# Turning the normalised residual: scaled rows and transposes in place of diagonal float32 matmuls

## The chip, the cores and the metric

The kernel runs on one core of a Trainium2 chip. The metric is the device time of one execution in microseconds (us); the time before is the median of three executions. A profile of one further execution gives the trace that the rows below come from. The engines are called PE (TensorE), DVE (VectorE), ACT (ScalarE), POOL (GpSimd) and SP (SyncE), as in the profile.

## The reference

One decoder layer over 2048 tokens of width 1024, all in float32. Two attention groups run side by side (stick-breaking attention with 8 heads, gated linear attention with 4), their outputs go through an output projection and are added to the residual, and a feed-forward part with a short convolution follows:

```
x = x + concat([o_sb, o_gla], axis=-1) @ w_out       # output projection, residual
h = rms_norm(x, ffn_norm_g)                          # x * rsqrt(mean(x*x) + 1e-6) * g
u = causal_depthwise_conv(h @ w_ffn_up, conv_w, conv_b)   # 1024 -> 5632, width 3
a, val = split(u, 2, axis=-1)
x = x + (silu(a) * val) @ w_ffn_down                 # 2816 -> 1024
return rms_norm(x, final_norm_g)
```

The change lies in how `h` is made from `x` and handed to the up-projection.

## The kernel before

**Precision.** Large products are computed with each float32 operand split into a high and a low part of type float32r (`split_psum` L92, `split_w` L101): ACT writes the high part out of PSUM (L94, or L97 with a scale per partition), and DVE writes the difference as the low part (L95, L98). A product is then three matmuls (high x high, high x low, low x high), as in the up-projection at L881 to L883, called ups here.

**Stages.** A first stage projects the input and stores queries, keys and values in DRAM. After it, `ffn(b, ...)` (L812) runs once for each of four blocks b of 512 tokens. For a block it runs the output projection (`accumulate`, L728), the norm and the turn to feature-major form (L839 to L854, the place of the change), the up-projection with convolution, and the down-projection (again `accumulate`).

**What runs between.** `ffn` is a generator. Each `yield` hands out an amount of the program's own clock, and a loop at the end of the kernel issues attention work for later blocks as that clock advances: one step of `attention_steps` (L506) whenever `done < clock / SPAN * total`, with SPAN = 1030 and total = 296. A step is, on PE, two matmuls that add to the attention output (acc, L581 and L582), four transposes of weights (tp, L566) and two matmuls for scores (z, L533); on ACT two sigmoids (into mt and wt) and the high part of the transposed weights (ws); on DVE a scan (L549), a product (L555) and the low part of ws (L95). Steps are used up before block 3's place of the change, so none stands there.

**Order.** PE's instructions stand in the order in which the program writes them (`manual_schedule` for PE). The order on DVE, ACT, POOL and SP is found by a scheduler from the dependencies. Engines wait for each other by semaphores. A tile that takes a named buffer (a `slot`, or one of the four PSUM banks of pool `pc` with tag "c") waits until the readers of the buffer's last tile are done.

**The place itself.** The last three rows of the output projection are staggered by token tile (128 tokens each): for t = 0 to 3, PE does the nine matmuls of tile t, DVE adds the residual into x1 (L786), ACT squares and sums the row (L789), DVE adds the two half sums (L795) and POOL raises the result to -0.5 (L799), which gives the scale r1 of tile t. After `yield FILL` (4.0), DVE multiplies the 128x128 identity by r1 for each t (dg, L846). Then, for each of the eight feature tiles k, PE multiplies the four x1 pieces (128 tokens x 128 features) with the four diagonal matrices (L851, plain float32), which scales and transposes them into one PSUM bank (tpu), and ACT and DVE write h2h and h2l from it, scaled by the feature gain g (L97, L98). h2h and h2l are two buffers each, of four feature tiles: slots 10 and 11, and 14 and 15. They are allocated once, in block 0. Each k ends with `yield 0.9`.

Of the kernel before, what the change touches and what calls it, by code (L numbers as in the profile page):

```python
# [8 lines left out]
F32 = mybir.dt.float32  # L9
F32R = mybir.dt.float32r  # L10
AF = mybir.ActivationFunctionType
ALU = mybir.AluOpType
# [4 lines left out]
P = 128  # L17
D = 1024
KT = D // P
S = 2048  # L20
TB = 512
# [29 lines left out]
def hybrid_block_kernel(ctx, tc, x, attn_norm_g, w_in, w_gate_up, b_gate_up, sb_out_g,  # L51
                        gla_out_g, w_out, ffn_norm_g, w_ffn_up, conv_w, conv_b,
                        w_ffn_down, final_norm_g, out):
    nc = tc.nc
# [4 lines left out]
    out = out[0]  # L59
# [4 lines left out]
    ident = const.tile([P, P], F32, name="ident")  # L64
# [27 lines left out]
    def split_psum(hi, lo, ps, scale=None):  # L92
        if scale is None:
            nc.scalar.activation(hi, ps, AF.Copy)  # L94
            nc.vector.tensor_tensor(out=lo, in0=ps, in1=hi.bitcast(F32), op=ALU.subtract)  # L95
        else:
            nc.scalar.activation(hi, ps, AF.Identity, scale=scale)  # L97
            nc.vector.scalar_tensor_tensor(out=lo, in0=ps, scalar=scale, in1=hi.bitcast(F32),  # L98
                                           op0=ALU.mult, op1=ALU.subtract)
# [10 lines left out]
    pc = ctx.enter_context(tc.tile_pool(name="pc", bufs=4, space=PSUM))  # L110

    def slot(n, shape, dtype, name):
        return big.tile(shape, dtype, tag=f"slot{n}", name=name)
# [4 lines left out]
    if True:  # L118
        c1.enter_context(tc.tile_pool(name="rpad", bufs=1, side="right")).tile([P, 24], F32, name="rpad")

        def w_tile(shape, dtype, name):
            return low.tile(shape, dtype, tag="w", name=name, bufs=4)
# [17 lines left out]
        for n in (6, 7, 8, 9, 10, 11, 14, 15, 0, 1, 2, 3, 4, 5, 12, 13):  # L140
            b, u = n // 4, n % 2
# [84 lines left out]
        with tc.tile_pool(name="lr", bufs=2, side="right") as lp, tc.tile_pool(name="lc", bufs=1, side="right") as lc:  # L226
# [16 lines left out]
            for b in range(NB):  # L243
# [11 lines left out]
                for j in range(NPAIR):  # L255
# [12 lines left out]
                                                 op0=ALU.mult, op1=ALU.add)  # L268
# [4 lines left out]
                                            in0=bcn[:, :, P - 1:P].to_broadcast([P, 4, P]), in1=bcn,  # L273
# [15 lines left out]
                                                   op0=ALU.mult, op1=ALU.mult)  # L289
# [127 lines left out]
        n = 0  # L417
# [270 lines left out]
    cc = ctx.enter_context(tc.tile_pool(name="cc", bufs=1))  # L688
# [13 lines left out]
    halo = [cc.tile([P, 2 * NCH, 2], F32, name=f"halo{i}") for i in range(2)]  # L702
    hadd = cc.tile([P, 2 * NCH, 2], F32, name="hadd")
    x1 = [slot(12 + u, [P, 2, D], F32, f"x1_{u}") for u in range(2)]
    h2h, h2l = [], []
    ur = Ring([w_tile([P, 2, KT, P], F32R, f"u{n}") for n in range(3)])
    d01 = w_tile([P, 2, 2, 512], F32R, "d01")
    dr = Ring([d01[:, 0], d01[:, 1], m1_tile([P, 2, 512], F32R, "d2")])
# [5 lines left out]
    def x1t(t):  # L714
        return x1[t // 2][:, t % 2, :]
# [96 lines left out]
    def ffn(b, oT, rows, nextT):  # L812
# [15 lines left out]
        if b == 0:  # L828
# [5 lines left out]
        rs1, rs2 = ([r[:, t:t + 1] for t in range(4)] for r in (r1, r2))  # L834
        last = b + 1 == NB
        yield from accumulate(oT, w_out, wou, b, squares=sq1, stagger=True, rstds=[r1], rows=rows,
                              extra=previous if b > 0 else remaining, first=None if b > 0 else ahead)
        if b == 0:
            h2h.extend(slot(10 + u, [P, 4, TB], F32R, f"h2h{u}") for u in range(2))  # L839
            h2l.extend(slot(14 + u, [P, 4, TB], F32R, f"h2l{u}") for u in range(2))  # L840
        yield FILL

        dgs = []
        for t in range(4):
            dg = cc.tile([P, P], F32, tag=f"dg{t}", name="dg")
            nc.vector.tensor_scalar(out=dg, in0=ident, scalar1=rs1[t], scalar2=None, op0=ALU.mult)  # L846
            dgs.append(dg)
        for k in range(KT):
            tp = pc.tile([P, 4, P], F32, tag="c", name="tpu")
            for t in range(4):  # L850
                nc.tensor.matmul(tp[:, t, :], x1t(t)[:, k * P:(k + 1) * P], dgs[t], start=True, stop=True)  # L851
            split_psum(h2h[k // 4][:, k % 4, :], h2l[k // 4][:, k % 4, :], tp.rearrange("p t q -> p (t q)"),
                       scale=g_f[:, k:k + 1])
            yield 0.9  # L854
        hcur, hprev = halo[b % 2], halo[(b + 1) % 2]
        if b > 0:
            nc.vector.tensor_tensor(out=hadd[:, :, 0], in0=hprev[:, :, 0], in1=cw[:, 0, :], op=ALU.mult)
# [6 lines left out]
        for gi, G in enumerate(GROUPS):  # L864
            gts = []
            for c in range(ch0, ch0 + G):
                cs = []
                for s in range(2):
# [17 lines left out]
                    n = s * NCH + c  # L886
# [73 lines left out]
    for b in range(NB):  # L960
        nextT = []
        for dt in ffn(b, oT, order if b == 0 else None, nextT):
            clock += dt
            while done < total and done < clock / SPAN * total:
                next(later, None)
                done += 1
        assert b + 1 == NB or done >= need[b + 1]
        oT = nextT
# [27 lines left out]
```

## Time and profile before

| | |
|---|---|
| median of three executions | 2766.29 us (2762.18 to 2768.05) |
| the profiled execution | 2762.93 us |
| its span in the trace | 2761.2 us |
| PE busy | 2696.3 us, 98% |
| DVE busy | 1686.7 us, 61% |
| ACT busy | 1146.3 us, 42% |
| POOL busy | 610.7 us, 22% |
| mean granted clock of PE | 0.996 |

The profiled execution is 1.7 us longer than its span; those lie around the instructions. The granted clock is a share of PE's full speed: 1.00 is the higher of its two levels (2.4 GHz), 0.50 the lower (1.2 GHz). The matmuls of PE overlap, and the duration given for one matmul is a latency; the distance between the starts of two neighbours says more.

### The profile page before, as it was taken

How to read it: one execution, taken by the hardware profiler on the slowest of the kernel's cores; microseconds unless marked ns; L12 is line 12 of the kernel's file. 1: busy time of each engine (PE TensorE's matmuls, PEld its weight loads, DVE VectorE, ACT ScalarE, POOL GpSimd, SP SyncE). 2: the span in 40 equal slices, each digit the busy share in tenths (PEclk: the TensorE clock that was granted, in tenths of full speed). 3: DMA queues.
4: the chain of work that ended last, by engine and by line, in shares of the span. 5: the costliest groups of instructions: out<-in, count | busy, mean ns of one | idle time of the engine just before them, and what ended most of it. 6: DMA issues, size and time to landing. Idle time of an engine off the chain costs nothing.

```text
span 2761.2 us, 36066 instructions
## 1 busy us (share of the span) xinstructions
PE 2696.3 (98%) x13000; PEld 2235.0 (81%) x13000; DVE 1686.7 (61%) x2777; ACT 1146.3 (42%) x2371; POOL 610.7 (22%) x937
## 2 busy tenths in 40 slices
PE   8999999999899899999999999999999999999998
PEld 7878888878688778887888888888888888888887
DVE  5246755457677687777776877777867334242333
ACT  5455533335465455554543444445434222220112
POOL 2001212214555555543111111111110000000000
PEclk9999999999999999999999999999999999999999
DMA  6215644477667677768455555574554656555552
GB/s 193 91 62 175 231 143 150 126 180 238 237 226 256 223 240 258 241 232 279 156 185 183 177 172 176 185 253 151 179 176 151 232 191 218 206 197 191 198 190 84
DMA packets 254563, 526.92 MB, mean 191 GB/s; under 512 B 54864, under 2 KB 143024, under 8 KB 231856
## 3 DMA queue, kind: packets, MB, share of 16 engines
q1 hardware_dynamic: 223136, 387.76, 42.8%
q0 software_dynamic: 31104, 136.33, 13.7%
q8 instruction: 102, 1.67, 0.2%
q14 instruction: 77, 0.63, 0.1%
q10 hardware_dynamic: 144, 0.52, 0.1%
HBM read 382.99 MB, written 141.56 MB: 190 GB/s over the span
## 4 chain that ended last, share of the span: by engine, by line
PE 85%; DVE 5%; DMA 4%; POOL 2%; ACT 2%; issue 2%; SPq 1%; ACTq 0%; POOLq 0%; DVEq 0%
PE ups L881 11%; PE ups L882 11%; PE ups L883 11%; PE d L760 6%; PE d L759 6%; PE d L761 6%; PE z L533 4%; PE tp L566 4%; PE mm L170 2%; PE mm L169 2%; PE mm L168 2%; PE acc L582 2%; PE mm L179 2%; PE mm L180 2%; PE mm L178 2%; PE acc L581 2%
## 5 line engine op out<-in xcount | busy, mean ns | idle before, releaser
L881 PE MATMUL ups<-h2h,u 128*128 128x512 f32 x1408 | 552.2, 392 | 3.9 <-DVE x L786 3.9
L882 PE MATMUL ups<-h2l,u 128*128 128x512 f32 x1408 | 551.0, 391 | 0.0
L883 PE MATMUL ups<-h2h,u 128*128 128x512 f32 x1408 | 550.3, 391 | 0.0
L881 PEld LDWEIGHTS ups<-h2h,u 128*128 128x128 f32 x1408 | 265.1, 188 | 60.5 <-DVE x L786 4.4
L883 PEld LDWEIGHTS ups<-h2h,u 128*128 128x128 f32 x1408 | 264.9, 188 | 57.2
L95 DVE TENSOR_TENSOR ws<-tp,ws 128x512 fp32r<-128x512 f32 (+1 forms) x320 | 193.8, 606 | 191.9 <-ACT ws L94 191.0
L882 PEld LDWEIGHTS ups<-h2l,u 128*128 128x128 f32 x1408 | 265.0, 188 | 55.5
L759 PE MATMUL d<-d,g 128*128 128x512 f32 x736 | 290.9, 395 | 4.2 <-DVE x L786 1.8
L94 ACT ACTIVATE ws<-tp 128x512 fp32r<-128x512 f32 (+1 forms) x320 | 170.2, 532 | 299.9 <-PE tp L566 295.5
L760 PE MATMUL d<-d,g 128*128 128x512 f32 x736 | 289.3, 393 | 1.5 <-POOL d L103 1.5
L761 PE MATMUL d<-d,g 128*128 128x512 f32 x736 | 288.7, 392 | 0.0
L893 DVE SCALAR_TENSOR_TENSOR ct<-ups,cwb,ct 128x511 f32<-128x511 f32 x176 | 131.7, 748 | 249.2 <-POOL ct L892 196.2
L888 ACT ACTIVATE ct<-ups,cwb 128x512 f32<-128x512 f32 x176 | 136.3, 775 | 340.3 <-PE ups L883 340.1
L549 DVE TENSOR_TENSOR_SCAN wtB<-mt,cy 128x512 f32<-128x512 f32 x192 | 248.4, 1294 | 3.1 <-ACT mt L538 3.0
L786 DVE TENSOR_TENSOR x<-d,x 128x512 f32<-128x512 f32 x128 | 85.8, 683 | 166.1 <-PE d L761 166.0
L892 POOL TENSOR_TENSOR ct<-ct,hadd 128x2 f32<-128x2 f32 x132 | 26.4, 200 | 688.7 <-ACT halo L890 324.5
L538 ACT ACTIVATE mt<-z 128x512 f32<-128x512 f32 (+2 forms) x320 | 170.5, 533 | 9.4 <-DVE cy L553 5.1
L759 PEld LDWEIGHTS d<-d,g 128*128 128x128 f32 x736 | 138.7, 189 | 36.0 <-DVE x L786 3.4
L760 PEld LDWEIGHTS d<-d,g 128*128 128x128 f32 x736 | 138.6, 188 | 31.8 <-POOL d L103 2.5
L761 PEld LDWEIGHTS d<-d,g 128*128 128x128 f32 x736 | 138.5, 188 | 30.9
L168 PE MATMUL mm<-hh,w 128*128 128x512 f32 x384 | 151.2, 394 | 0.0
L170 PE MATMUL mm<-hh,w 128*128 128x512 f32 x384 | 149.4, 392 | 0.8 <-POOL w L103 0.8
(262 smaller groups left out, 5375.4 us busy)
## 6 DMA issues: line engine op xcount, KB each, us to landing
u<-wup SPq DMA_DIRECT2D x132, 1024.0 KB, 4.7
d<-wdn SPq DMA_DIRECT2D x94, 512.0 KB, 3.4
wup<-u POOLq DMA_DIRECT2D x44, 1024.0 KB, 6.6
kvA<-kvs POOLq DMA_DIRECT2D x52, 512.0 KB, 4.8
uraw<-in_w_ffn_up_dram SPq DMA_DIRECT2D x44, 512.0 KB, 4.6
wdn<-d POOLq DMA_DIRECT2D x44, 512.0 KB, 5.2
d<-wou SPq DMA_DIRECT2D x38, 512.0 KB, 4.3
dw<-wdn SPq DMA_DIRECT2D x38, 512.0 KB, 4.2
```

What stands on the lines that cost most here:

```text
L94: nc.scalar.activation(hi, ps, AF.Copy)
L95: nc.vector.tensor_tensor(out=lo, in0=ps, in1=hi.bitcast(F32), op=ALU.subtract)
L168: nc.tensor.matmul(ps, whi[k][:, fs], hh[b][k // 4][:, k % 4, :], start=(k == 0), stop=False)
L170: nc.tensor.matmul(ps, wlo[k][:, fs], hh[b][k // 4][:, k % 4, :], start=False, stop=(k == KT - 1))
L538: nc.scalar.activation(m[:, lo:TB], z[:, :width], AF.Sigmoid, scale=-0.125)
L549: nc.vector.tensor_tensor_scan(out=pp[:, ::-1], data0=mr, data1=mr, initial=1.0 if prev is None else prev, op0=ALU.mult, op1=ALU.bypass)
L759: nc.tensor.matmul(accs[t], gh[:, ts], whi, start=(ci == 0), stop=False)
L760: nc.tensor.matmul(accs[t], gh[:, ts], wlo, start=False, stop=False)
L761: nc.tensor.matmul(accs[t], gw[:, ts], whi, start=False, stop=(ci == G - 1))
L881: nc.tensor.matmul(ps, whi[:, k, :], hk, start=(k == 0), stop=False)
L882: nc.tensor.matmul(ps, whi[:, k, :], lk, start=False, stop=False)
L883: nc.tensor.matmul(ps, wlo[:, k, :], hk, start=False, stop=(k == KT - 1))
```

## The change

The identity is no longer scaled. DVE instead scales the residual rows themselves: for each token tile t and each half u of the 1024 features, x1 is multiplied by r1 of the tile into a new tile xn[u] (128x512 float32, eight instructions a block). PE then transposes the 128x128 pieces of xn with the identity, and `split_psum` follows as before. Three further things move with it:

- xn[0] and xn[1] take slots 11 and 15, which before held h2h's and h2l's second half. The second half of h2h and h2l is therefore allocated anew in each block, and it waits until the transposes of the xn in its slot have been done.
- For the first four feature tiles, PE does the transposes of token tiles 0 to 2 first, twelve of them into all four banks of `pc`, and those of token tile 3 behind them. `split_psum` of each of the four tiles follows on its last transpose.
- The yields are 4.0, 1.3, 0.5 and four times 0.5, where they were 4.0 and eight times 0.9.

```
-        if b == 0:
-            h2h.extend(slot(10 + u, [P, 4, TB], F32R, f"h2h{u}") for u in range(2))
-            h2l.extend(slot(14 + u, [P, 4, TB], F32R, f"h2l{u}") for u in range(2))
+        h2h = [slot(10, [P, 4, TB], F32R, "h2h0"), None]
+        h2l = [slot(14, [P, 4, TB], F32R, "h2l0"), None]
+
+        xn = [slot(n, [P, 4, D // 2], F32, f"xn{u}") for u, n in enumerate((11, 15))]
+        for t in range(4):
+            for u in range(2):
+                nc.vector.tensor_scalar(out=xn[u][:, t, :], in0=x1t(t)[:, u * 512:(u + 1) * 512], scalar1=rs1[t],
+                                        scalar2=None, op0=ALU.mult)
         yield FILL
 
-        dgs = []
-        for t in range(4):
-            dg = cc.tile([P, P], F32, tag=f"dg{t}", name="dg")
-            nc.vector.tensor_scalar(out=dg, in0=ident, scalar1=rs1[t], scalar2=None, op0=ALU.mult)
-            dgs.append(dg)
-        for k in range(KT):
-            tp = pc.tile([P, 4, P], F32, tag="c", name="tpu")
-            for t in range(4):
-                nc.tensor.matmul(tp[:, t, :], x1t(t)[:, k * P:(k + 1) * P], dgs[t], start=True, stop=True)
+        def turn(tp, k, ts_):
+            for t in ts_:
+                nc.tensor.transpose(tp[:, t, :], xn[k // 4][:, t, (k % 4) * P:(k % 4 + 1) * P], ident)
+
+        def parts(tp, k):
             split_psum(h2h[k // 4][:, k % 4, :], h2l[k // 4][:, k % 4, :], tp.rearrange("p t q -> p (t q)"),
                        scale=g_f[:, k:k + 1])
-            yield 0.9
+
+
+        tps = [pc.tile([P, 4, P], F32, tag="c", name="tpu") for _ in range(KT // 2)]
+        for k, tp in enumerate(tps):
+            turn(tp, k, range(3))
+        yield 1.3
+        for k, tp in enumerate(tps):
+            turn(tp, k, (3,))
+            parts(tp, k)
+        h2h[1] = slot(11, [P, 4, TB], F32R, "h2h1")
+        h2l[1] = slot(15, [P, 4, TB], F32R, "h2l1")
+        yield 0.5
+        for k in range(KT // 2, KT):
+            tp = pc.tile([P, 4, P], F32, tag="c", name="tpu")
+            turn(tp, k, range(4))
+            parts(tp, k)
+            yield 0.5
```

How the instructions stand now is shown for block 2. The number behind a name tells tiles of one name apart. In the program before, PE's order from the last attention step ahead of the turn into the turn is this: the end of a step (its two acc matmuls, four transposes tp, two score matmuls z), then four diagonal matmuls for each feature tile, four tiles in a row (the first two are shown whole here).

```order
L581 MATMUL acc_16466<-ws0_5042,kvA_5057 128x512
L582 MATMUL acc_16466<-ws0_5042,kvA_5057 128x512
L566 MATMUL tp_16846<-ident_60,wtC_5513 128x128 x2
L566 MATMUL tp_16846<-ident_60,wtA_5055 128x128 x2
L533 MATMUL z_16855<-kvA_5057,qA_5058 128x128 x2
L851 MATMUL tpu_16876<-dg_16868,x1_0_6295 128x128
L851 MATMUL tpu_16876<-dg_16870,x1_0_6295 128x128
L851 MATMUL tpu_16876<-dg_16872,x1_1_6296 128x128
L851 MATMUL tpu_16876<-dg_16874,x1_1_6296 128x128
L851 MATMUL tpu_16883<-dg_16868,x1_0_6295 128x128
L851 MATMUL tpu_16883<-dg_16870,x1_0_6295 128x128
```

Behind the fourth tile, before, another whole step stands on PE, and then the other four tiles. Now, behind the step, PE has the twelve and the four transposes of feature tiles 0 to 3, two tiles from xn1, a step, the last two tiles, and the first ups matmul (L897, which was L881):

```order
L849 MATMUL tpu_16850<-ident_60,xn0_16822 128x128 x3
L849 MATMUL tpu_16851<-ident_60,xn0_16822 128x128 x3
L849 MATMUL tpu_16848<-ident_60,xn0_16822 128x128
L849 MATMUL tpu_16849<-ident_60,xn0_16822 128x128
L849 MATMUL tpu_16850<-ident_60,xn0_16822 128x128
L849 MATMUL tpu_16851<-ident_60,xn0_16822 128x128
L849 MATMUL tpu_16878<-ident_60,xn1_16823 128x128 x4
L849 MATMUL tpu_16885<-ident_60,xn1_16823 128x128 x4
L581 MATMUL acc_16526<-ws1_5043,kvA_5057 128x512
L582 MATMUL acc_16526<-ws1_5043,kvA_5057 128x512
```

The step that stood behind the fourth tile stands behind the sixth now, and all sixteen transposes of the first four tiles are in one piece ahead of it. On DVE, before, the stretch from the low part of the transposed weights (ws0) to the first h2l of block 2 reads so (r1 is the sum of squares of the last token tile):

```order
L95 TENSOR_TENSOR ws0_5042<-tp_16830,ws0_5042 128x512
L795 TENSOR_TENSOR r1_16341<-sq1_16340 128x1
L549 SCALAR_TENSOR_TENSOR wtB_5056<-mt1_5035,cy_16691 128x512
L846 TENSOR_SCALAR dg_16874<-ident_60,r1_16341 128x128
L555 TENSOR_TENSOR wtC_5513<-wtC_5513,wtB_5056 128x512
L95 TENSOR_TENSOR ws1_5043<-tp_16846,ws1_5043 128x512
L549 SCALAR_TENSOR_TENSOR wtB_5056<-mt0_5034 128x128
L98 SCALAR_TENSOR_TENSOR h2l0_6810<-tpu_16876,g_f_6285,h2h0_6808 128x512
```

And now, from the residual sum x1_1 of the last token tile's second half to the first h2l (L785 and L794 are the lines that were L786 and L795):

```order
L785 TENSOR_TENSOR x1_1_6296<-d3_16592,x1_1_6296 128x512
L843 TENSOR_SCALAR xn0_16822<-x1_1_6296,r1_16305 128x512
L843 TENSOR_SCALAR xn1_16823<-x1_1_6296,r1_16305 128x512
L555 TENSOR_TENSOR wtA_5055<-wtA_5055,wtB_5056 128x512
L95 TENSOR_TENSOR ws0_5042<-tp_16806,ws0_5042 128x512
L794 TENSOR_TENSOR r1_16305<-sq1_16304 128x1
L549 SCALAR_TENSOR_TENSOR wtB_5056<-mt1_5035,cy_16663 128x512
L843 TENSOR_SCALAR xn0_16822<-x1_1_6296,r1_16305 128x512
L843 TENSOR_SCALAR xn1_16823<-x1_1_6296,r1_16305 128x512
L555 TENSOR_TENSOR wtA_5055<-wtA_5055,wtB_5056 128x512
L95 TENSOR_TENSOR ws1_5043<-tp_16834,ws1_5043 128x512
L549 SCALAR_TENSOR_TENSOR wtB_5056<-mt0_5034,cy_16694 128x512
```

Behind the last of these stand one more product (L555) and the first h2l. The small dg has gone; two scalings of 128x512 stand in its place, two more ahead of ws0, and the scan behind ws1 is a full one of 512 columns, where a scan of 128 stood.

## Rows read from the trace of the kernel before

**Rows 1.** Page, busy time of the engines: busy us (share of span) xinstructions.

```profile
PE 2696.3 (98%) x13000; PEld 2235.0 (81%) x13000; DVE 1686.7 (61%) x2777; ACT 1146.3 (42%) x2371; POOL 610.7 (22%) x937
```

**Rows 2.** Windows (us; busy of PE, PEld, DVE, ACT, POOL; PEclk; DMA; GB/s).

```profile
746.87:764.22 17.35, 13.42 (x98) 11.84 (x97) 17.11 (x25) 12.89 (x25) 10.62 (x12) 1.00 0.50 167
...
1330.67:1344.57 13.90, 12.72 (x97) 11.55 (x96) 12.37 (x25) 10.59 (x21) 5.09 (x9) 1.00 0.42 148
...
1896.24:1909.49 13.25, 12.52 (x98) 11.30 (x96) 12.95 (x24) 10.05 (x21) 2.97 (x7) 1.00 0.61 197
...
2383.38:2392.77 9.39, 7.58 (x65) 7.20 (x64) 5.84 (x10) 5.45 (x9) 1.03 (x2) 1.00 0.45 164
```

**Rows 3.** Lines by form: count | busy us, mean ns | idle us before, releaser.

```profile
L566 PE MATMUL tp<-ident,wtA 128*128 128x128 f32 x520 | 97.6, 273 | 1.6 <-DVE wtA L555 1.6
...
L851 PE MATMUL tpu<-dg,x 128*128 128x128 f32 x256 | 30.9, 276 | 4.3 <-DVE dg L846 4.3
...
L549 DVE TENSOR_TENSOR_SCAN wtB<-mt,cy 128x512 f32<-128x512 f32 x192 | 248.4, 1294 | 3.1 <-ACT mt L538 3.0
...
L95 DVE TENSOR_TENSOR ws<-tp,ws 128x512 fp32r<-128x512 f32 x224 | 153.8, 687 | 169.1 <-ACT ws L94 168.3
...
L555 DVE TENSOR_TENSOR wtA<-wtA,wtB 128x512 f32<-128x512 f32 x107 | 77.8, 727 | 5.1 <-DVE wtB L549 0.9
...
L98 DVE SCALAR_TENSOR_TENSOR h2l<-tpu,g_f,h2h 128x512 fp32r<-128x512 f32 x32 | 23.0, 743 | 2.5 <-ACT h2h L97 1.3
...
L383 DVE TENSOR_SCALAR og<-po,grr 128x128 f32<-128x128 f32 x64 | 19.4, 344 | 12.0 <-POOL grr L89 11.9
...
L264 DVE TENSOR_SCALAR la<-mm,bgate 128x512 f32<-128x512 f32 x8 | 6.0, 746 | 13.6 <-ACT e L260 13.6
```

**Rows 4.** One line's instructions, L846: count, min/median/max ns, first and last start.

```profile
L846 DVE TENSOR_SCALAR dg<-ident,r x16: 256/278/1497, 739.3 to 2385.9; 128x128 f32<-128x128 f32 x16
```

**Rows 5.** Timeline, blocks 1 and 3: start us, us, engine, work [idle before <-releaser].

```profile
1339.15 1.45 ACT L97 ACTIVATE h2h<-tpu,g_f 128x512 fp32r<-128x512 f32 x2
...
2385.93 0.29 DVE L846 TENSOR_SCALAR dg<-ident,r 128x128 f32<-128x128 f32 x1 [0.66 <-POOL r L799]
...
2386.80 0.69 ACT L97 ACTIVATE h2h<-tpu,g_f 128x512 fp32r<-128x512 f32 x1 [1.72 <-PE tpu L851]
```

**Rows 6.** Timeline of block 2, around the diagonal matmuls.

```profile
1898.26 0.68 DVE L95 TENSOR_TENSOR ws<-tp,ws 128x512 fp32r<-128x512 f32 x1
...
1899.00 0.50 PE L582 MATMUL acc<-ws,kvA 128*128 128x512 f32 x1 [0.51 <-DVE ws L95]
...
1902.01 0.73 DVE L98 SCALAR_TENSOR_TENSOR h2l<-tpu,g_f,h2h 128x512 fp32r<-128x512 f32 x1
...
1903.52 0.48 PE L581 MATMUL acc<-ws,kvA 128*128 128x512 f32 x1
...
1904.06 0.38 PE L566 MATMUL tp<-ident,wtA 128*128 128x128 f32 x2
...
1904.74 2.84 PE L851 MATMUL tpu<-dg,x 128*128 128x128 f32 x24
...
1907.19 2.06 DVE L98 SCALAR_TENSOR_TENSOR h2l<-tpu,g_f,h2h 128x512 fp32r<-128x512 f32 x3
```

**Rows 7.** Timeline of block 0, around the last dg.

```profile
753.35 1.50 DVE L846 TENSOR_SCALAR dg<-ident,r 128x128 f32<-128x128 f32 x1
...
753.48 1.27 POOL L103 TENSOR_TENSOR d<-draw,d 128x512 fp32r<-128x512 f32 x1
...
754.90 3.17 PE L851 MATMUL tpu<-dg,x 128*128 128x128 f32 x26 [2.47 <-DVE dg L846]
```

**Rows 8.** Timeline of block 0, an ups matmul behind an idle time of PE.

```profile
947.57 0.50 PE L881 MATMUL ups<-h2h,u 128*128 128x512 f32 x1 [3.94 <-DVE x L786]
```

**Rows 9.** Windows behind two idle times of PE, columns as in rows 2.

```profile
948.00:952.00 4.00, 4.00 (x13) 3.14 (x12) 3.40 (x6) 0.00 (x0) 2.50 (x4) 0.60 0.93 320
...
755.00:759.00 4.00, 4.00 (x34) 3.86 (x35) 3.88 (x6) 2.95 (x5) 0.57 (x1) 1.00 0.96 305
```

More of the change, by code (lines that the diff above doesn't have):

```diff
@@ L704, in hybrid_block_kernel @@
     x1 = [slot(12 + u, [P, 2, D], F32, f"x1_{u}") for u in range(2)]
-    h2h, h2l = [], []
     ur = Ring([w_tile([P, 2, KT, P], F32R, f"u{n}") for n in range(3)])
```

## The prediction

> **What bounds the kernel now.** I read the page first: TensorE (PE) is busy for 98% of the span [rows 1], so in most places a microsecond of PE work taken away is a microsecond won. The change touches one place only, which comes four times, once per block of 512 tokens: the turn of the normalised residual into feature-major operands, between the last output-projection matmul and the first up-projection matmul (ups). So next I cut those four stretches out of the trace [rows 2]. Each label runs from the issue of the first PE instruction behind the last projection matmul to the issue of the first ups matmul. The reader is to see three things there. The stretches last 17.35, 13.90, 13.25 and 9.39 us, 53.9 together. PE idles in them for 3.9, 1.2, 0.7 and 1.8 us (length less busy time). And VectorE (DVE) is busy for 17.11 of 17.35, 12.37 of 13.90 and 12.95 of 13.25 us in the first three: in this place two engines are full, not one. Block 3 has no attention work left to run beside it, and there DVE has 3.5 us of air.
>
> **What is removed: PE time.** The diagonal matmuls are 8 x 4 per block, 128 in the program, but the trace has 256 of them [rows 3]: a float32 matmul runs as two passes. 24 take 2.84 us [rows 6]; the last one's 0.27 us of modelled tail off, that is 2.57/23 = 0.112 us each, so 256 x 0.112 = 28.6 us. A transpose is one instruction: two in 0.38 us [rows 6] is a pitch of 0.38 - 0.27 = 0.11 us (the means of 273 and 276 ns in [rows 3] are latencies and hide this). 128 x 0.11 = 14.1 us. So PE loses 14.5 us of work, 3.6 per block. If nothing came back, that would be the gain.
>
> **What is added: DVE time.** Four small scalings per block (dg, median 278 ns [rows 4]) give way to eight of 128x512. No row shows such an instruction from SBUF to SBUF. Upper bound: the same operation out of PSUM, 746 ns for 512 columns and 344 for 128 [rows 3]. These differ by 402 ns over 384 columns, 1.05 ns each. But dg, SBUF to SBUF, took 278 for 128, 66 ns or 63 such columns under 344, as if its columns went two at a time; with half the slope 512 columns cost 278 + 201 = 479 ns, my lower bound and, being the same form, my value. Starts follow each other 0.08 us closer than durations (three h2l in 2.06 us at a mean of 743 ns [rows 3, 6]), so a block's scalings cost 8 x 0.40 against 4 x 0.20: +2.4 us of DVE per block, on an engine that is full in three of them.
>
> **What the new order makes late.** PE now runs sixteen transposes into four PSUM banks in 1.75 us and then needs a bank back for the fifth tile. A bank is free when ScalarE (h2h, 0.69 us; two back to back take 1.45, one every 0.76 [rows 5]) and then DVE (h2l, 0.74 us) have read it. Before, PE needed 8 x 0.112 = 0.89 us per tile and had attention steps between tiles, so the banks were free in time. Now PE waits at DVE's pace, with fewer steps to cover it. The program's own count of the place falls from 4.0 + 8 x 0.9 = 11.2 to 4.0 + 1.3 + 0.5 + 4 x 0.5 = 7.8, and a step goes out every 1030/296 = 3.5 of that count, so in blocks 0 to 2 three steps stand in the stretch instead of four; the order shows it. A step costs PE 1.22 us (1903.52 to 1904.74 [rows 6]) wherever it stands, so an end that stays the same with one step fewer is a loss of 1.22. The moved work issues no DMA, and passes none on the queues of SP and POOL.
>
> Block 2, step by step. The scalings of tokens 0 and 1 push the third one's back by 0.2 us and this tile's own two cost 0.85, so the copy ws that starts at 1898.26 starts 1.1 later, and the PE matmul that waits for it (1899.00, idle 0.51 [rows 6]) goes at 1900.0. PE finishes that step, the twelve and the four transposes at 1902.7. By the order, between that ws and the first h2l DVE has a scan (1.2), two scalings (0.9), a product (0.6), ws (0.6), a scan (1.2) and a product (0.6; means of [rows 3] less the 0.08): first h2l at 1905.1 instead of 1902.01 [rows 6]. PE idles 3.2 us, then turns tiles 5 and 6 as banks come (to 1907.05), runs a step (to 1908.3) and tiles 7 and 8 (to 1909.2). Ups needs tile 5's bank, whose h2l stands behind a ws (which waits for ScalarE until 1908.9) and another scan: read at 1911.45. Ups at 1911.5 against 1909.49: +2.0, and +1.2 for the missing step: **+3.2**.
>
> Block 1, in the same way: the step's ws goes 1.1 later, the first h2l stands behind two small scans and ScalarE's work on an attention step, PE idles 2.4 us for the fifth tile, and ups comes at 1344.95 against 1344.57 with one step fewer: **+1.6**. Block 0: here PE waited 2.47 us for the last dg [rows 7]. The last scaling is ready about as late (755.0), but twelve transposes stand ahead of the wait, not six passes; the rest runs at h2l's pace, and ups comes near 761.6 against 764.22 less 1.2 for the step that is missing: **-1.5**. Block 3: the chain sum of squares, power, scaling, PE stays. The last scaling ends 0.2 later than dg did (2385.93 + 0.48 instead of + 0.29 [rows 5]), ScalarE starts at 2386.9 instead of 2386.80 and needs 8 x 0.76 instead of 8 x 0.89, and ups waits for tile 5's bank, freed when DVE, released by the eighth tile's transposes (its output takes the slot that they read), has done the fifth h2l: 2392.3 against 2392.77, **-0.5**. Were the scalings 0.75 us long, the last sum would wait half a us for DVE, and this term would be +0.3. The sum is +2.8, of which the PE saving of 14.5 is a part: 17 us of new waits stand against it.
>
> **The clock.** New idle on PE has a second price. After an idle of 3.94 us (PE's last before 947.57) the granted clock was 0.60 over the next 4 us [rows 8, 9], that is, mostly the lower of the two levels, 1.2 GHz; after 2.47 us at 754.90 it stayed at 1.00 [rows 7, 9]. At 0.60 the 4 us did 2.4 us of work at full clock: a fall costs 1.6. Blocks 1 and 2 get idles of 2.4, 3.2 and 2.3 us. I count one fall, +1.6. All together +4.4.
>
> **Reference points.** The profiled execution took 2762.93 us, the median of the three runs is 2766.29, 3.4 above it. I put the difference on the median: 2766.3 + 4.4 = 2770.7. A measurement of this kernel tells no change from one of up to 0.2% (5.5 us).
>
> **Contention, weighed against a rule.** In block 0 one dg took 1.50 us instead of 0.28; it began at 753.35, a POOL subtraction ran from 753.48 to 754.75, and dg ended 0.1 us behind it [rows 7]. So a scaling can be held by POOL. The Trainium skill (SBUF — State Buffer, section "SBUF: two separate sides") says that VectorE in a two-port mode and GpSimd take a shared port pair as an exclusive lock for a whole instruction; this row agrees. By the rule the eight scalings of block 0 stand exposed to three such subtractions instead of four dgs: at 1.2 us each the sum would be up to 3.6 us higher; by the rows one of sixteen was caught, and I leave it in the range.
>
> **Rivals.** Faster (25%): the PE saving comes through. It needs DVE to hand back banks early, for which the 3.5 us of air in block 3 and the 3.9 us of idle PE in block 0 speak; against it DVE's 89 to 99% in the first three blocks. Half of the 14.5 us kept gives 2759, all of it 2752.
> Slower by over 0.2% (29%): one mechanism, the clock. If each stretch's idle in front of ups makes PE's clock fall (from somewhere over 2 us of idle, by the rows), ups starts at half speed four times: +2.8 + 4 x 1.6 = +9.2, 2775.5. It decides from the third fall on. For it: three of the four stretches get idles of 2 us or more. Against: 2.47 us did not do it.
> That a transpose is also two passes, and the PE saving is not there, would give 2770.7 + 14.5 = 2785. But where the order has two attention transposes the trace has two records (1904.06 [rows 6]): I give it nothing.
>
> **How the numbers follow.** My own case holds 46%: the waits eat the saving, the sum lies between +2.8 with no fall of the clock and +6.0 with two, and contention and the changed neighbourhood of the attention steps move it by some 3 us either way; 2766 to 2774 is its own range. Its upper end passes the 0.2% line (2771.8), for which I take 5 of the 46. With the rivals whole on their sides that makes faster 0.25, same 0.41, slower 0.34. The range reaches from somewhat below the half-kept saving to four falls with some contention: 2756 to 2779.
>
> **What would show it.** Right: 128 transposes at a pitch of 0.11 us where 256 passes stood; scalings of 0.48 us; in block 2, PE waiting 3 us for h2l ahead of the fifth tile and 2 us ahead of ups; the four stretches, with 1.22 us added to each of the first three, at 16, 15.5, 16.5 and 8.9 us. Wrong: h2l starting within 1 us of h2h in blocks 1 and 2, so that PE never idles over 1 us there; a scaling of 0.75; or granted clocks of 0.5 behind each stretch.

## The result and the profile after

The changed kernel is slower: 2785.29 us, median of six executions (2774.69 to 2791.30), against 2766.67 of the kernel before (2762.18 to 2768.78), a ratio of 1.0061, 95% interval 1.0044 to 1.0079. Timed again after the experiments it gave 2774.66 against 2766.51, ratio 1.0042 (1.0023 to 1.0061). So, by the two ratios, it costs 0.4 to 0.6%, 12 to 17 us. The forecast was slower by 4.4 us, 2770.7, with a range up to 2779.

The page of the profiled execution (2786.51 us), busy time by engine, answers to [rows 1]:

```profile
span 2784.8 us, 35828 instructions
...
PE 2698.2 (97%) x12872; PEld 2232.8 (80%) x12872; DVE 1693.9 (61%) x2793; ACT 1145.7 (41%) x2371; POOL 615.1 (22%) x937
```

PE has 128 records fewer, as forecast, but is busy 1.9 us longer. The same work took longer somewhere, and not only in the place of the change. I matched PE instructions that stand in the same order in both programs, and took the difference of their start times, after less before:

| PE instruction | after - before, us |
|---|---|
| first projection matmul of block 0 | +7.5 |
| first of the projection's second half, block 0 | +11.6 |
| first ups of block 0 | +10.4 |
| last down-projection matmul of block 0 | +14.2 |
| first ups of block 1 | +17.3 |
| first ups of block 2 | +19.3 |
| last down-projection matmul of block 2 | +23.1 |
| first ups of block 3 | +22.2 |
| end of span | +23.6 |

About a third, 7.5 of 23.6 us, is lost before block 0's output projection even begins, in a part of the program that the change does not touch. (Not every row is the change's doing: between the first ups of block 0 and its last down-projection matmul the two programs have the same attention steps, and the loss of 3.8 us there has no cause shown.) PE's timeline ahead of the projection has one large wait. Before, and then after (start us, us, work, idle before and releaser):

```profile
576.11 0.61 PE L533 MATMUL z<-qk 128*128 128x384 f32 x2 [2.71 <-ACT wtA L540]
```

```profile
583.63 0.69 PE L533 MATMUL z<-qk 128*128 128x384 f32 x1 [8.35 <-ACT wtA L540]
```

ACT's wtA is late because ACT stood behind a gate activation that waited 20.2 us, not 13.6, for a store. SP's issues show why. In them osc<-ge is the store of a gated output, ge<-gon a load into a buffer that such a store frees, and uraw the weights of the up-projection. Before:

```profile
565.07 0.43 SPq L452 DMA_DIRECT2D osc<-ge  x1
570.48 0.32 SPq L448 DMA_DIRECT2D ge<-gon  x1
...
649.13 2.40 SPq L875 DMA_DIRECT2D uraw<-in_w_ffn_up_dram  x2
```

After, SP's issues in the same place, and ACT's wait, after and then before:

```profile
566.37 0.99 SPq L891 DMA_DIRECT2D uraw<-in_w_ffn_up_dram  x2
567.45 1.43 SPq L452 DMA_DIRECT2D osc<-ge  x1
578.98 0.34 SPq L448 DMA_DIRECT2D ge<-gon  x1
```

```profile
579.07 0.60 ACT L449 ACTIVATE ge<-mm 128x512 f32<-128x512 f32 x1 [20.24 <-DMA osc<-ge]
```

```profile
570.57 0.60 ACT L449 ACTIVATE ge<-mm 128x512 f32<-128x512 f32 x1 [13.62 <-DMA osc<-ge]
```

The loads, the store behind them, and the same store before (issuing engine, count, KB each, median us from issue to landing; windows 564:569):

```profile
uraw<-in_w_ffn_up_dram SPq DMA_DIRECT2D x2, 512.0 KB, 8.3
...
osc<-ge SPq DMA_DIRECT2D x1, 256.0 KB, 11.5
```

```profile
osc<-ge SPq DMA_DIRECT2D x1, 256.0 KB, 5.4
```

The first two loads of up-projection weights, 1 MB, are issued 83 us earlier than before, ahead of a gate store that ScalarE waits for. The store lands after 11.5 us, not 5.4. The next issue on SP, which waits for that store, comes 11.5 us behind it (578.98 less 567.45), where it came 5.4 us behind it (570.48 less 565.07).

The four stretches of [rows 2] look like this after (same columns):

```profile
756.96:774.58 17.62, 12.25 (x61) 9.84 (x60) 15.98 (x22) 11.74 (x22) 8.38 (x9) 0.81 0.47 164
1345.36:1361.86 16.50, 11.25 (x57) 9.40 (x55) 12.04 (x27) 9.78 (x21) 4.43 (x9) 0.79 0.38 126
1913.10:1928.77 15.67, 10.36 (x58) 8.07 (x56) 14.14 (x22) 10.47 (x19) 4.16 (x4) 0.89 0.49 157
2405.75:2414.94 9.19, 5.63 (x33) 4.04 (x32) 6.06 (x12) 5.71 (x10) 1.03 (x2) 0.83 0.43 166
sum 58.98, PE 39.49 PEld 31.35 DVE 48.22 ACT 37.70 POOL 17.99; mean PE 9.87 PEld 7.84 DVE 12.05 ACT 9.43 POOL 4.50
```

The reader is to see two things. Together they are 5.1 us longer than before (58.98 against 53.89), although the first three hold one attention step less each. And the granted clock, 1.00 in all four before, is 0.79 to 0.89: part of each stretch ran at the lower level, and PE is idle for 3.6 to 5.4 us of each. In block 2 the waits stand where they were forecast, ahead of the last step's acc (for ws), of the fifth tile and of ups; the middle one is 1.61 us where 3 was forecast, the last 2.06 where 2 was. The sixteen transposes took 2.62 us where 1.75 was worked out, in part at the lower clock:

```profile
1916.76 0.65 PE L582 MATMUL acc<-ws,kvA 128*128 128x512 f32 x1 [1.42 <-DVE ws L95]
...
1918.91 2.62 PE L849 MATMUL tpu<-ident,xn 128*128 128x128 f32 x16
1923.15 1.31 PE L849 MATMUL tpu<-ident,xn 128*128 128x128 f32 x8 [1.61 <-DVE h2l L98]
...
1928.77 0.47 PE L897 MATMUL ups<-h2h,u 128*128 128x512 f32 x1 [2.06 <-DVE h2l L98]
```

### The profile page after: what moved, and what is told of

Same layout as the page of the kernel before. It is cut to its first block, busy times and chain, and to the rows that moved or that the text cites. A ratio compares the mean times of both kernels' runs of the same rounds, so it can differ in the third digit from the quotient of the medians.

```text
span 2784.8 us, 35828 instructions
## 1 busy us (share of the span) xinstructions
PE 2698.2 (97%) x12872; PEld 2232.8 (80%) x12872; DVE 1693.9 (61%) x2793; ACT 1145.7 (41%) x2371; POOL 615.1 (22%) x937
## 4 chain that ended last, share of the span: by engine, by line
PE 86%; DVE 5%; DMA 4%; issue 2%; ACT 2%; POOL 1%; SPq 0%; ACTq 0%; POOLq 0%; DVEq 0%
PE ups L897 11%; PE ups L898 11%; PE ups L899 11%; PE d L759 7%; PE d L758 6%; PE d L760 6%; PE z L533 4%; PE tp L566 4%; PE mm L170 3%; PE mm L168 3%; PE mm L169 3%; PE acc L582 2%; PE mm L179 2%; PE mm L178 2%; PE mm L180 2%; PE acc L581 2%
## 5 line engine op out<-in xcount | busy, mean ns | idle before, releaser
L897 PE MATMUL ups<-h2h,u 128*128 128x512 f32 x1408 | 552.4, 392 | 3.9 <-DVE h2l L98 3.9
L897 PEld LDWEIGHTS ups<-h2h,u 128*128 128x128 f32 x1408 | 265.2, 188 | 60.9 <-DVE h2l L98 2.4
L785 DVE TENSOR_TENSOR x<-d,x 128x512 f32<-128x512 f32 x128 | 86.2, 684 | 164.9 <-PE d L760 164.8
L538 ACT ACTIVATE mt<-z 128x512 f32<-128x512 f32 (+2 forms) x320 | 170.7, 533 | 11.3 <-DVE cy L553 5.1
L168 PE MATMUL mm<-hh,w 128*128 128x512 f32 x384 | 151.3, 394 | 0.0
L169 PE MATMUL mm<-hl,w 128*128 128x512 f32 x384 | 150.2, 391 | 0.0
```

Of the source, the lines that this page charges most:

```text
L168: nc.tensor.matmul(ps, whi[k][:, fs], hh[b][k // 4][:, k % 4, :], start=(k == 0), stop=False)
L169: nc.tensor.matmul(ps, whi[k][:, fs], hl[b][k // 4][:, k % 4, :], start=False, stop=False)
L538: nc.scalar.activation(m[:, lo:TB], z[:, :width], AF.Sigmoid, scale=-0.125)
L897: nc.tensor.matmul(ps, whi[:, k, :], hk, start=(k == 0), stop=False)
```

## The experiments

Two questions: are the moved loads part of the loss, and how do the turns come to their length? Each run is timed against the kernel before on the same chip; a ratio compares the two. The times of one kernel scatter by some 10 us either way here (before: 2756 to 2777 over all its executions), so ratios have intervals of some 0.15% to either side, and traces carry the rest. A trace is one execution, and the chance falls of the clock are in it too.

**The moved loads.** dg stood in pool cc with four tiles of 512 bytes per partition. Without them the pools behind cc begin 2 KB lower, among them the buffers of uraw. The first run puts the 2 KB back and leaves all else of the change.

```
+    cc.tile([P, 4, P], F32, name="ccpad")
```

> The changed kernel with 2 KB of unused tile put where the dg tiles stood in pool cc, so that the pools behind it keep the addresses they had before; the only thing that moves on any engine against the changed kernel is that SP issues the first two loads of up-projection weights (uraw) where it issued them before, behind the gate stores, not ahead of them. Theory A (about half of the loss comes from these two loads, 1 MB, getting in front of a 256 KB store that ScalarE and then PE wait for at 565 to 584 us, and from what follows on the loads up to 726): the changed kernel loses 11.6 of its 23.6 us before the second half of block 0's projection, so this run comes 9 to 12 us under the changed kernel, near 2775, and PE's wait ahead of the z matmul at 576 us is 2.7 us again, not 8.4. Theory B (the early difference is chance, and the loss is all in the four turns and the clock): no change, 2785.

Measured: 2773.72, ratio 1.0021 (1.0007 to 1.0035). The wait at the z matmul:

```profile
579.20 0.62 PE L533 MATMUL z<-qk 128*128 128x384 f32 x2 [3.70 <-ACT wtA L540]
```

It is short again, and the time is the one that theory A named; theory B's 2785 is out. The second run does the reverse to the kernel before.

```
-            dg = cc.tile([P, P], F32, tag=f"dg{t}", name="dg")
+            dg = sm.tile([P, P], F32, tag=f"dg{t}", name="dg", bufs=1)
```

> The kernel before with its dg tiles taken from the pool sm, which is opened later, so that pool wu moves down by 2 KB; the diagonal matmuls stay, and only the first two uraw loads move on SP, to where the changed kernel has them. Theory A: 9 to 12 us slower than before, near 2777, with a PE wait of about 8 us ahead of the z matmul at 576 us. Theory B: as before, 2767, within 3 us.

Measured: 2772.07, ratio 1.0016 (1.0001 to 1.0032): slower with the diagonal matmuls untouched, though by half of what theory A said. The z matmul came at 580.92 us, 4.8 late, but its own wait was only 3.37 us, not 8, and the store behind the two loads landed after 6.1 us. PE was late before the loads were issued at 566: its granted clock was 0.72 from 545 to 557 us, where it was 1.00 before. So this trace does not show the wait of theory A. It stands in the two traces of the changed kernel (store 11.5 and 10.6 us, wait 8.35 and 7.84): the early loads do not delay the store as much each time. The third run holds the two loads back by order alone, with the changed addresses.

```
+                        with tc.issue_after(draws[1]):      # the second draw load on SP
+                            nc.sync.dma_start(out=raw, in_=wuv[:, s, :, c * P:(c + 1) * P])
```

> The changed kernel without the pad: addresses as changed, but the first two uraw loads are told to stay behind the second load of output-projection weights on SP, which is where they stood before. No other instruction moves on any engine. If the order on SP is what cost the time (theory A), this comes out like the pad, 2771 to 2777. If the addresses themselves matter (another theory: the tiles behind cc lie elsewhere, and reads or writes collide otherwise), it stays near 2785.

Measured: 2770.19, ratio 1.0015 (0.9997 to 1.0032); the z matmul waits 3.1 us. So the wait comes from the order on SP, not from the addresses as such; the time is clear of the changed kernel's first measurement, not of its second. That the addresses set this order is shown by the first two runs; which earlier tile the lower buffers no longer wait for is not shown.

How much is it? Over the traces, block 0's first projection matmul comes 4.9 to 7.5 us later than before in the three with early loads (this second run and the changed kernel twice), and 0.7 to 4.1 in the ten others with late loads; the means, with before at 0, are 6.5 and 2.1. So 4.4 us, which is the 0.16% of the second run. This is an estimate with the clock in it, as the second run's trace shows. The next term of the table, +4.1 up to the second half of the projection, is not the loads': this piece takes 26.8 to 36.9 us over the traces, with both orders at both ends.

**Steps in the turn.** With the pad, the yields were raised so that four steps stand in the turns again.

```
-        yield 1.3
+        yield 2.4
...
-        yield 0.5
+        yield 1.6
...
-            yield 0.5
+            yield 0.8
```

> As the changed kernel with the pad, with the yields of the turn raised to 4.0 + 2.4 + 1.6 + 4 x 0.8 = 11.2, the count before, so that four attention steps stand in the turns of blocks 0 to 2 again. Theory C (in the turns PE idles for 2 to 3 us ahead of the fifth tile and of ups, and the granted clock falls for it, 12 us of clock lost in and right behind the four turns): steps that fill the waits take away most of the falls of blocks 0 to 2, 4 to 8 us under the pad alone. Theory D (DVE is the bound there, and each step brings DVE work along, so the waits only grow): within 2 us of the pad alone.

Measured: 2769.83, ratio 1.0014 (1.0000 to 1.0029), 3.9 us under the pad by the medians, just short of theory C's 4, and the clock still fell in three turns. The ratios of the two overlap: undecided by time. In the traces the three steps more cost the four stretches nothing: they sum to 59.39 us, with the pad alone to 59.42.

**Scaled rows and transposes alone.** With the pad, the twelve-and-four order is given up: four transposes per feature tile, 0.9 after each, as the diagonal matmuls had it.

```
-        for k, tp in enumerate(tps):
-            turn(tp, k, range(3))
-        yield 1.3
...
+        for k in range(KT):
+            if k == KT // 2:
+                h2h[1] = slot(11, [P, 4, TB], F32R, "h2h1")
+                h2l[1] = slot(15, [P, 4, TB], F32R, "h2l1")
+            tp = pc.tile([P, 4, P], F32, tag="c", name="tpu")
+            turn(tp, k, range(4))
+            parts(tp, k)
+            yield 0.9
```

> As the changed kernel with the pad, but the transposes in the order of the diagonal matmuls before, all four token tiles of a feature tile together, with 0.9 after each: scaled rows and transposes alone. Theory C (the sixteen transposes into four banks in one piece ahead of the steps make the waits): less idle ahead of the fifth tile, clock falls fewer, 3 to 8 us under the pad alone. Theory D (DVE's scalings and h2l set the pace whatever the order): like the pad alone within 3 us. If the PE saving of 3.6 us a block came through here it would be near 2755.

Measured: 2768.35, ratio 1.0002 (0.9988 to 1.0017): level with before, 5.4 us under the pad by the medians; the intervals of the two overlap. This kernel has before's steps and before's loads, so its turns can be compared with before's directly, and the next three runs vary it in one thing each. The first gives PE its 256 instructions back.

```
-            for t in ts_:
+            for t in [*ts_, *ts_]:                # each transpose twice, same place
```

> As the scaled rows with transposes tile by tile and the pad (2768.35), with each transpose issued twice into the same place, so that PE has 256 again as it had passes of diagonal matmuls: 14 us of PE work put back. If the saving of PE work in the turns buys nothing because PE waits there for the banks anyway and then runs at a lower clock (theory C), putting it back costs nothing: within 3 us of 2768, and if the work keeps the clock up, even up to 4 us under. If the saving came through and was lost elsewhere, 14 us over, 2782.

Measured: 2785.16, ratio 1.0068 (1.0052 to 1.0084), 16.8 over. Theory C as I had put it, that PE's work is free there, falls: the saving does come through. The next doubles DVE's added work.

```
+                for _ in range(2):
                     nc.vector.tensor_scalar(out=xn[u][:, t, :], ...)
```

> As the scaled rows with transposes tile by tile and the pad (2768.35), with each scaling issued twice, which adds eight of about 0.4 us a block to DVE, 3.2 us a block and 12.8 in all. Theory D (DVE is full in the turns, so its work counts there): 6 to 12 us over, 2774 to 2780. Theory C: the scalings of the first three token tiles are hidden, only the last tile's second pair counts, 0.8 us a block: 3 us over, near 2771.

Measured: 2777.92, ratio 1.0043 (1.0026 to 1.0060), 9.6 over by the medians and 11.3 by the ratios, for 12.8 us of DVE work. Theory D: most of DVE's added work counts in the turns. Two things are mixed in. Two of the scalings of block 0 stood beside subtractions on POOL and took 1.43 and 2.02 us, some 2.5 us more than the others:

```profile
L845 DVE TENSOR_SCALAR xn<-x,r x64: 455/481/2020, 735.2 to 2401.3; 128x512 f32<-128x512 f32 x64
```

And the turn of block 3 grew too, from 9.23 to 11.55 us, where DVE is not full: there the work stands in the chain that PE waits for. The third moves half of the scalings to ScalarE.

```
+                else:
+                    nc.scalar.activation(xn[u][:, t, :], xs, AF.Copy, scale=rs1[t])
```

> As the scaled rows with transposes tile by tile and the pad (2768.35), but ScalarE does the scalings of the second half of the features (an activation with the scale r1), so DVE has four instead of eight a block. If DVE's load ahead of the first h2l sets the turns of blocks 0 to 2 (theory D), four scalings of 0.4 us less on DVE take 1 to 1.6 us from each of these turns, and the run comes 3 to 5 us under, near 2764. If the turns are set by the chain through the last sum of squares and the banks (theory C), no change, within 2 us; and if ScalarE is then late with h2h and ws, up to 3 us over.

Measured: 2761.69, ratio 0.9989 (0.9975 to 1.0003), under by 6.7 us by the medians and by 3.6 (0.13%) by the ratios, where theory D said 3 to 5; the intervals of the two overlap. The sums of the four stretches, of the tile-by-tile kernel, with transposes twice, with scalings twice, and with half of the scalings on ScalarE, in this order (sum of the lengths, then busy times):

```profile
sum 58.96, PE 40.05 PEld 32.17 DVE 51.28 ACT 41.06 POOL 19.51; mean PE 10.01 PEld 8.04 DVE 12.82 ACT 10.26 POOL 4.88
```

```profile
sum 71.00, PE 54.58 PEld 48.12 DVE 53.82 ACT 43.46 POOL 19.44; mean PE 13.64 PEld 12.03 DVE 13.46 ACT 10.87 POOL 4.86
```

```profile
sum 71.27, PE 43.53 PEld 35.51 DVE 62.84 ACT 41.58 POOL 22.37; mean PE 10.88 PEld 8.88 DVE 15.71 ACT 10.39 POOL 5.59
```

```profile
sum 53.98, PE 37.60 PEld 27.59 DVE 47.59 ACT 46.38 POOL 19.33; mean PE 9.40 PEld 6.90 DVE 11.90 ACT 11.60 POOL 4.83
```

Read them against 53.89 of before. With as many PE instructions as before the turns are 17.1 us longer (71.00): that is the price of scaled rows in this trace, waits and lower clock together. Halving the instructions gives 12.0 of it back (58.96). The transposes do save; in the traces the scaled rows cost more. How much of the 17.1 is clock is open: length times the clock's shortfall is 10.3 us in the four turns of the one and 8.5 in the other, and none before. And these are single traces: one turn of the changed kernel differs by 2.3 us between two of them, and the tile-by-tile kernel, 5.1 us longer in the turns, is level by time.

**The shared slot.** xn takes the slot of the second h2l, so DVE cannot start it before the eighth tile's transposes, and ups waits for the fifth bank. A buffer of its own for the fifth low part, where the pad was, takes this away.

```
-    cc.tile([P, 4, P], F32, name="ccpad")
+    h2l4 = cc.tile([P, TB], F32R, name="h2l4")      # used for k == 4
```

> As the scaled rows with transposes tile by tile (2768.35, ratio 1.0002), with the low part of the fifth feature tile in a buffer of its own (2 KB, where the pad stood) in place of a quarter of slot 15, so that DVE may read the fifth bank while the transposes of the eighth tile still read xn in that slot. Theory S (the shared slot makes ups wait 0.8 to 1.3 us in every turn: DVE does not start the second four h2l before the last transposes): the wait ahead of the first ups goes, 1 us a turn, 3 to 5 us under, ratio near 0.999. Theory D (DVE has other work ahead of these h2l anyway): no change within 1 us.

Measured: 2765.43, ratio 1.0008 (0.9993 to 1.0022). PE's first ups matmul of a product, all 1408, idle before them, in the tile-by-tile kernel and now:

```profile
L891 PE MATMUL ups<-h2h,u 128*128 128x512 f32 x1408 | 553.4, 393 | 8.8 <-DVE h2l L98 5.2 <-DVE x L786 3.7
```

```profile
L894 PE MATMUL ups<-h2h,u 128*128 128x512 f32 x1408 | 552.9, 393 | 2.4 <-DVE x L786 2.2 <-DVE h2l L98 0.2
```

The wait for h2l goes from 5.2 to 0.2 us, and the four stretches sum to 53.76: the mechanism of theory S is shown. The time does not show it: 2.9 us under by the medians, 0.06% over by the ratios. Both together, ScalarE and the buffer:

```
+                    nc.scalar.activation(xn[u][:, t, :], xs, AF.Copy, scale=rs1[t])
+    h2l4 = cc.tile([P, TB], F32R, name="h2l4")
```

> As the kernel with half of the scalings on ScalarE (2761.69, ratio 0.9989), with the same buffer for the fifth low part. Theory S: in its trace PE waits 0.83, 1.27, 1.28 and 0.91 us for h2l ahead of the first ups, 4.3 us in all; without them 3 to 4 us under it, ratio near 0.9975, faster than both kernels. Theory D: 0.9989 again.

Measured: 2761.20, ratio 0.9985 (0.9970 to 1.0001). Theory S's 3 to 4 us under the run with ScalarE alone did not come: 0.5 by the medians, 0.04% by the ratios, though the waits for h2l ahead of ups fell from 4.3 to 1.5 us. It is the fastest of all, well under the changed kernel; against the kernel before its gain of 0.15% is just not clear of noise. The next run has the changed kernel's order and four steps, and is otherwise this one, which its text calls e10:

```
-        for k in range(KT):
+        for k, tp in enumerate(tps):
+            turn(tp, k, range(3))
+        yield 2.4
...
```

> As e10, but with the last token tile's transposes last, as in the changed kernel, and four steps in the turn (2.4 + 1.6 + 4 x 0.8). If the order with the last token tile last takes nothing by itself once the steps are back, within 2 us of e10; if sixteen transposes in one piece let PE wait for the banks (theory C), 3 to 6 us over e10.

Measured: 2764.44, ratio 1.0002 (0.9988 to 1.0016), 3.2 over by the medians; the intervals overlap, so the order of the transposes is not settled as a cost by itself.

**The changed kernel again**, with no edit, to see whether its two parts add.

> The changed kernel once more, unaltered, to size the two parts: the pad alone left it at a ratio of 1.0021 to before, and the two moved loads alone, put into the kernel before, gave 1.0016. If the two parts add, the changed kernel comes at 1.0037, near 2776; if the loads cost more where the turn is changed as well, or the difference of 11.6 us between the changed kernel and the pad holds as first measured, at 1.006, near 2782.

Measured: 2774.66, ratio 1.0042, near the sum of 1.0021 and 1.0016. The first measurement, 1.0061, lies above that sum, which stays open: its interval and this one overlap. The two differ in the clock that was granted: a mean of 0.9887 over the first six executions and 0.9906 over these nine, 5.3 us of the span, which is what the ratios differ by. This second measurement also overlaps the pad's interval. Only the two measurements of the changed kernel together (mean 1.0052) stand clear of the two runs that hold the loads late (1.0021 and 1.0015): 0.34%, some 9 us, an estimate.

## Why the prediction was wrong

Two steps failed. The first is one sentence: "The moved work issues no DMA, and passes none on the queues of SP and POOL." I argued it from the diff. The order of SP says otherwise: taking four small tiles out of a pool moved two loads of 512 KB past the gate stores. It is worth 4.4 us by the second run and some 9 by the changed kernel against the runs with late loads, both estimates, in a part of the program where I had set the change to nothing. With 4.4 the forecast would have been 2775.1. The second is "I count one fall, +1.6": the clock fell in every turn of the first profile, and the turns came 5 to 6 us longer in the traces than worked out. The loads and the clock are not separated further, and what is left of the first measurement's 17 us stays open.

The turn alone, without that, is the pad's run: +0.21%, and +0.15% by order alone, 4 to 6 us by the ratios (intervals from -1 to 10), where I had said +4.4. That the sum was about right is partly luck: its terms were less so.

- **PE time removed.** Right in count, 128 instructions for 256. Ten in 1.31 us, less the tail of 0.27, is a pitch of 0.116 us against 0.11. At the lower clock they took longer: sixteen in 2.62 us in block 2, 0.157 apart, which the sum had at 1.75.

```profile
2407.09 1.31 PE L849 MATMUL tpu<-ident,xn 128*128 128x128 f32 x10 [0.96 <-DVE xn L843]
```

- **DVE time added.** Right: a median of 480 ns against 479, none held by POOL (at most 520). The upper bound was not the same operation, as I said: the 746 ns of L264 [rows 3] are an addition and a minimum in one instruction. The row of the scaling, as in [rows 4]:

```profile
L843 DVE TENSOR_SCALAR xn<-x,r x32: 453/480/520, 751.1 to 2408.7; 128x512 f32<-128x512 f32 x32
```

- **"17 us of new waits stand against it."** Near in size, by the runs with transposes twice and once, 17.1 of cost and 12.0 given back, but that is partly luck: the measured 17.1 hold up to 10.3 of lower clock, mine held none.
- **The turns one by one.** With 1.22 us for each missing step they were 18.84, 17.72, 16.89 and 9.19 in the first profile, where 16, 15.5, 16.5 and 8.9 were forecast: 62.6 against 56.9. The second profile has 62.0, the pad's 63.1. So in the traces the turns cost 8 to 9 us over before, where +2.8 was worked out and +4.4 with the clock. The two turns that a trace of these shows at the full clock came near: block 1 of the changed kernel's second profile, 14.24 + 1.22 = 15.46 for 15.5, and block 3 of the pad, 8.53 for 8.9. Here is that block 1; in the first profile it took 16.50 at 0.79, with DVE, ACT and POOL as busy as here, so the 2.3 us more are the clock's.

```profile
1343.95:1358.19 14.24, 8.54 (x57) 6.54 (x55) 12.03 (x27) 9.77 (x21) 4.41 (x9) 1.00 0.43 144
```

- **The clock.** I counted one fall, +1.6. (Two would already have passed the 0.2% line, 2.8 + 3.2 against 5.5, not only three.) Every turn of the first profile and three of the second have one. Length times the clock's shortfall (17.62 x 0.19 and so on) is 10.1 us in the first profile and 6.7 in the second; waits at the lower clock cost nothing, so these are upper bounds. The slower rival had the clock fall in front of every ups. It fell earlier, inside the turns, and behind them ups ran at 1.00 in blocks 0 to 2 of the first profile. It fell in turns whose single waits were shorter than I had allowed: 1.42, 1.61 and 2.06 us in block 2. The 2.47 us in one piece at 754.90 [rows 7, 9] were a poor measure of what a turn with several waits does.
- **The missing steps.** The three steps are paid late, in block 2, as the 1.22 each said: the table's +3.8 between ups of block 2 and its end.
- **Contention.** None of the changed kernel's 32 scalings was held, but a scan on the path was. Before, the first scan of block 0's turn ended just ahead of POOL's subtractions. Now two scalings stand in front of it and push it beside them: it took 2.30 us, not 1.23 (a later one 2.23, mean 1294 ns [rows 3]), and PE's wait for the ws behind it grew from 1.24 to 3.06 us. I had block 0 at -1.5; with its missing step it came at +1.5. These rows agree in kind with the rule of the Trainium skill that was weighed (SBUF — State Buffer, section "SBUF: two separate sides"). After, and then before:

```profile
757.46 3.52 POOL L103 TENSOR_TENSOR d<-draw,d 128x512 fp32r<-128x512 f32 x2
...
757.62 2.30 DVE L549 TENSOR_TENSOR_SCAN wtB<-mt 128x512 f32<-128x512 f32 x1
...
762.25 0.50 PE L582 MATMUL acc<-ws,kvA 128*128 128x512 f32 x1 [3.06 <-DVE ws L95]
```

```profile
746.51 1.23 DVE L549 TENSOR_TENSOR_SCAN wtB<-mt 128x512 f32<-128x512 f32 x1
...
747.79 3.03 POOL L103 TENSOR_TENSOR d<-draw,d 128x512 fp32r<-128x512 f32 x2
...
750.35 0.51 PE L582 MATMUL acc<-ws,kvA 128*128 128x512 f32 x1 [1.24 <-DVE ws L95]
```

The range's upper end, 2779, was set by the clock and contention alone, since no term stood for work outside the four places.

## What to carry to other kernels

When a change adds or drops a tile, compare the order of every queue over the whole program, DMA issues first, not only around the edit: an allocation can move a load far away from it, and a load put ahead of a store that someone waits for can cost what it delays. In a place where a second engine is full, price a saving on the first together with the work that it hands to the second: here, in the traces, 12 us saved on PE met 17 us of cost. Where an engine gets several short waits in a row, count the lower clock in each such place.

## What the runs showed of the hardware

A store of 256 KB issued right behind two loads of 512 KB took 11.5, 10.6 and 6.1 us to land in three traces (the changed kernel's two and the second run's), where the same store took 5.4 before. Two executions of one program differed by 2.3 us in one turn with DVE, ACT and POOL equally busy (16.50 us at 0.79, 14.24 at 1.00). The scatter of whole executions goes with the clock too: the kernel before took 2756.1 us at a mean granted clock of 0.997 and 2776.57 at 0.992. A scan of 128x512 took 1.23 us in block 0 before, and 2.30 where it began just behind a subtraction on POOL. And a scaling of 128x512 float32 from SBUF to SBUF took 480 ns; an addition and minimum of that size in one instruction, out of PSUM, took 746 [rows 3].
